# A two-block network on one core: loads of W and raw products spaced by task steps, 512-column pairs in the first expert matrix, a W build with two PSUM tiles per step, a later key transposition

## The chip, the cores and the metric

The kernel runs on one core of a Trainium2 chip. The metric is the device time of one execution in microseconds (us). Before the change three executions gave 3197.25, 3197.32 and 3201.41 us, a median of 3197.32 us. Engines are named as in the profile: PE (TensorE), PEld (its weight loads), DVE (VectorE), ACT (ScalarE), POOL (GpSimd), SP (SyncE, which here only issues DMAs).

## The reference, cut to what matters

256 tokens of width 2048 go through a block with stick-breaking attention and a squared-ReLU MLP, and then through a block with a pooled and a sparse attention, a product-key expert layer and a gate. All of it is float32. The change is in the second block, in its key projections and above all in the expert layer:

```
qkv, gates, u = split(rmsnorm(x) @ w_in)                   # keys are normed per head
q   = xn @ w_q                                             # 8 heads x 2 x 128
s   = einsum(q, sub_keys); top 16 x top 16 -> 16 experts per head and token: idx, g = softmax
h   = gelu(einsum('td,thkd->thk', xn, u_tab[idx]))         # u_tab: 16384 x 2048
out = einsum('thk,thkd->td', g * h, v_tab[idx])            # v_tab: 16384 x 2048
```

The kernel gathers nothing. It multiplies all 16384 experts with all tokens, and puts the routing weights g into a dense matrix W (16384 experts x 256 tokens, zero where an expert is not chosen): out = (W * gelu(xn u_tab^T)) v_tab.

## The kernel before

**Precision by splitting.** Every weight matrix comes in tiles of 128x2048 float32 (1 MB, tile name raw, three buffers). Each tile has two halves of 1024 columns. For each half ACT writes a rounded copy `hi` (L1431) and DVE, or in some stretches for every second half POOL, writes the rest `lo = raw - hi` (L1433); there are four buffers of hi and of lo. The left operand is split likewise (xh, xl, both in the tile xx). A product then is hi*xh + hi*xl + lo*xh, three passes over PE.

**Two shapes of product.** In `xs_half` (L240) the tokens are the stationary operand and 512 weight columns move; the accumulators are `acc`. In `ws_half` the weights are stationary, 128x128 at a time, and the tokens move; the accumulator is one PSUM bank named `ws`. `ws_half` has two forms. With `wide` unset, each of the 8 k-steps of a half issues three matmuls of 256 columns: hi on xh (L252), hi on xl (L253), lo on xh (L254). With `wide` set it issues one matmul of 512 columns (hi on xh and xl side by side, L250) and one of 256 (lo on xh, L254); the two halves of the bank are then added when it is emptied. The first MLP matrix (w1) uses the wide form already, the first expert matrix (peer_u, 128 items of one raw tile each) does not.

**What sets the order.** The order of the instructions of each engine is that in which the Python code issues them. The main loop walks over the halves. Before half n it issues hi and lo of half n+3 (`advance`); then the matmuls of half n. Twice in each half, in its middle and at its end, it calls `hook()`, in which each waiting task (a generator) goes on to its next `yield`. One such call is a **step** here, so a half has two. A half's load of a new raw tile is issued on SP as soon as the last lo of the tile in that buffer has been issued, so SP's queue holds it behind what was issued earlier.

**The expert layer's tasks**, all stepped that way:

- `u_item`: after the two halves of an item of peer_u, ACT copies its bank into a slot (L1264), 8 items to a slot; the slot is written to DRAM as raw product `gd` (L1270). Slots are ten buffers of 1 MB (names slot), handed out in the order in which they came free.
- `build`/`batch`: while peer_u runs, W is made from one-hot matrices, 8 tokens per batch, 32 batches, five steps apart. A batch is 16 matmuls of 128x128 in float16 into two `tp` banks (L1212), which ACT copies to a slot (L1216); two batches make a slot, which is written to DRAM as `wd` (L1221).
- `loader`: when W is complete, it reads for each of 16 groups of 1024 experts the piece of W and the raw products back into slots (L1232), both in one step, and marks the group as loaded 14 steps later. At most two groups are loaded and unused.
- `acts`: for a loaded group it multiplies by the norm factor (DVE L1281), applies gelu (ACT L1283), multiplies by W (DVE, two L1248), splits the result into ah (ACT L1291) and al (DVE L1293). These come one step after the other: DVE in one step, ACT in the next, DVE in the next.

The second expert matrix (peer_v) uses ah and al as stationary operand, in the form of L240, 16 groups after each other. `acts` of the first three groups run while peer_u is still being multiplied.

**The key transposition.** `kv_one` takes the accumulators of a key and value projection: DVE scales the keys into the tile xg (`spread`, L581), ACT copies the values (L615), and one step later PE transposes xg (L621).

**PSUM.** Eight banks are shared by kinds; `caps` says how many of each kind may be in use.

Of the kernel before, what the change touches and what calls it, by code (L numbers as in the profile page):

```python
# [19 lines left out]
P = 128  # L20
D = 2048
T = 256
# [4 lines left out]
def tile_two_blocks(ctx, tc, a, out):  # L27
    nc = tc.nc
    PE, ACT, DVE, POOL, SP = nc.tensor, nc.scalar, nc.vector, nc.gpsimd, nc.sync
# [10 lines left out]
    def f32(ap):  # L40
        return ap.bitcast(F32)

    live, caps = {}, {"acc": 4, "ws": 3, "tp": 3}
    idle, used = deque(range(8)), []

    def full(kind):
        return live.get(kind, 0) >= caps[kind] or kind in ("acc", "ws", "tp") and not idle

    def bank(kind):
        live[kind] = live.get(kind, 0) + 1  # L50
        i = idle.popleft()
        t = psp.tile([P, 512], F32, tag=f"bank{i}", name=kind)
        used.append((t, kind, i))
        return t

    def take(kind):
        while full(kind):
            hook()
        return bank(kind)

    def get(kind):
        while full(kind):
            yield
        return bank(kind)

    def tmp(pool, shape, dt, tag, cap):
        caps[tag] = cap
        while full(tag):
            yield
        live[tag] = live.get(tag, 0) + 1  # L70
        return pool.tile(shape, dt, tag=tag, name=tag, bufs=cap)

    def put(*kinds):
        for k in kinds:
            if not isinstance(k, str):
                u = next(u for u in used if u[0] is k)
                used.remove(u)
                idle.append(u[2])
                k = u[1]
            live[k] -= 1  # L80
# [18 lines left out]
    def S(ap, fn):  # L99
        seq.append(("s", ap, fn))  # L100
# [9 lines left out]
    st = {"rate": 2, "n": 0, "norm": 0, "rok": False, "pool_lo": False, "nb": 0, "nW": 0}  # L110
# [35 lines left out]
    def flush():  # L146
        until(lambda: st["norm"] == 0)
# [96 lines left out]
    def ws_half(hi, lo, k0, b, wide):  # L244
        xx, p = st["xx"], b[:, :T]
        for kk in range(8):
            k = k0 + kk
            c = slice(kk * P, (kk + 1) * P)
            if wide:
                PE.matmul(b, hi[:, c], xx[:, k].rearrange("p a t -> p (a t)"), start=k == 0, stop=False)  # L250
            else:
                PE.matmul(p, hi[:, c], xx[:, k, 0], start=k == 0, stop=False)  # L252
                PE.matmul(p, hi[:, c], xx[:, k, 1], start=False, stop=False)  # L253
            PE.matmul(p, lo[:, c], xx[:, k, 0], start=False, stop=k == 15)  # L254
            if kk == 3:
                hook()
# [18 lines left out]
    def ws_item(ap, evac, wide=False):  # L275
        box = {}

        def fn(j, hi, lo):
            if j == 0:
                box[0] = take("ws")  # L280
            else:
                flush()
            ws_half(hi, lo, 8 * j, box[0], wide)
            if j == 1:
                tasks.append(evac(box[0]))
        S(ap, fn)
# [276 lines left out]
    def rms64(tt, p, ng):  # L563
        sc = st["r"][:, tt:tt + 1]
        j0 = yield from tmp(ph["ew"], [P, 512], F32, "xn", 2)
        j = j0[:, :ng * 64]
        ACT.activation(j, p, AF.Square, scale=sc)
        yield
        r = smp.tile([P, 8], F32, tag="r64", name="r64", bufs=4)
        DVE.tensor_reduce(r[:, :ng], j.rearrange("p (g d) -> p g d", d=64), axis=AX.X, op=ALU.add)  # L570
        put("xn")
        DVE.tensor_scalar(r[:, :ng], r[:, :ng], 1.0 / 64, 1e-6, op0=ALU.mult, op1=ALU.add)
        yield
        POOL.tensor_tensor(r[:, :ng], r[:, :ng], mhalf[:, 0:1].to_broadcast([P, ng]), op=ALU.pow)
        yield
        DVE.tensor_scalar(r[:, :ng], r[:, :ng], sc, None, op0=ALU.mult)
        return r

    def spread(p, r):
        x = yield from tmp(smp, [P, 4, P], F32, "xg", 2)  # L580
        DVE.tensor_tensor(x.rearrange("p g (d e) -> p g d e", d=2),  # L581
                          p.rearrange("p (g e) -> p g e", g=4).unsqueeze(2).to_broadcast([P, 4, 2, 64]),
                          r.unsqueeze(2).unsqueeze(3).to_broadcast([P, 4, 2, 64]), op=ALU.mult)
        return x
# [25 lines left out]
    def kv_one(br, tt, p):  # L610
        while "E" not in done:
            yield
        r = yield from rms64(tt, p[:, :256], 4)
        x = yield from spread(p[:, :256], r[:, :4])
        ACT.activation(ph["VS"][:, tt, br], p[:, 256:], AF.Copy, scale=st["r"][:, tt:tt + 1])  # L615
        put(p)
        yield
        w = ph["qkw"][:, 1:2]
        b = yield from get("tp")
        for g in range(4):  # L620
            PE.transpose(b[:, g * P:(g + 1) * P], x[:, g], ident)  # L621
        put("xg")
        yield
        sl = (slice(None), br, slice(None), slice(tt * P, (tt + 1) * P))
        bv = b.rearrange("p (a b) -> p a b", a=4)
        ACT.activation(ph["kh"][sl], bv, AF.Copy, scale=w)
        yield
        DVE.scalar_tensor_tensor(ph["kl"][sl], bv, w, f32(ph["kh"][sl]), op0=ALU.mult, op1=ALU.subtract)
        put(b)
        done.add(("k", br, tt))  # L630
# [377 lines left out]
    def drop(nm):  # L1008
        del st[nm]
        w, i = held.pop(nm)  # L1010
        free[w].append(i)
# [181 lines left out]
    def batch(tb, h, S):  # L1193
        tm = ph["tm"]
        ts = slice(tb * 16 + h * 8, tb * 16 + h * 8 + 8)
        A = yield from tmp(tm, [P, 8, P], F16, "A", 2)
        DVE.tensor_tensor(A, ph["io16"].unsqueeze(1).to_broadcast([P, 8, P]),
                          ph["I2T"][:, ts].unsqueeze(2).to_broadcast([P, 8, P]), op=ALU.is_equal)
        yield
        eq = tm.tile([P, P, 8], F16, tag="eqb", name="eqb", bufs=1)  # L1200
        DVE.tensor_tensor(eq, ph["io8"], ph["I1T"][:, ts].unsqueeze(1).to_broadcast([P, P, 8]), op=ALU.is_equal)
        B = tm.tile([P, 2, P, 8], F16, tag="B", name="B", bufs=2)
        for m in range(2):
            DVE.tensor_tensor(B[:, m], eq, ph[f"G{m + 1}"][:, ts].unsqueeze(1).to_broadcast([P, P, 8]), op=ALU.mult)
            yield
        yield
        Sv = S.rearrange("p a t -> p (a t)").rearrange("p (i t) -> p t i", t=16)
        for k0 in (0, 4):
            bk = yield from get("tp")
            for k in range(4):  # L1210
                for m in range(2):
                    PE.matmul(bk[:, k * P:(k + 1) * P], B[:, m, :, k0 + k], A[:, k0 + k], start=m == 0, stop=m == 1)  # L1212
            if k0:
                put("A")
            yield
            ACT.copy(Sv[:, h * 8 + k0:h * 8 + k0 + 4], bk.rearrange("p (t i) -> p t i", t=4))  # L1216
            put(bk)
        st["nb"] = st.get("nb", 0) + 1
        st["nS", tb] = st.get(("nS", tb), 0) + 1
        if st["nS", tb] == 2:  # L1220
            SP.dma_start(st["wd"][:, :, tb].rearrange("g p c -> p g c"),  # L1221
                         S.rearrange("p a t -> p (a t)").rearrange("p (g c) -> p g c", g=16))
            drop(("S", tb))

    def loader():
        while "W" not in done:
            yield
        for g in range(16):
            while st["nW"] > 1 or nfree() < 2 + 2 * st["nW"] or ("u", g) not in done:
                yield  # L1230
            for nm, d in (("W", st["wd"][g].rearrange("p b c -> p (b c)")), ("ge", st["gd"][g])):
                SP.dma_start(grab((nm, g), keep=9).rearrange("p a t -> p (a t)"), d)  # L1232
            st["nW"] += 1
            for _ in range(14):
                yield
            done.add(("Wl", g))

    def wv(g, j0, n):
# [18 lines left out]
    def u_item(g, j):  # L1257
        def evac(b):
            if j == 0:
                while nfree() < 1:  # L1260
                    yield
                grab(("raw", g), keep=9)
            r = st["raw", g]
            ACT.copy(r[:, j], b[:, :T])  # L1264
            put(b)
            if j == 7:
                if g == 0:
                    st["gd"] = drp.tile([16, P, 8 * T], F32, name="gd")
                yield
                SP.dma_start(st["gd"][g], r.rearrange("p a t -> p (a t)"))  # L1270
                drop(("raw", g))
                done.add(("u", g))
        ws_item(a["peer_u"][8 * g + j], evac)

    def acts():
        for g in range(16):
# [281 lines left out]
```

## Time and profile before

| what | before |
|---|---|
| median of three executions | 3197.32 us |
| the profiled execution | 3201.31 us, span of the core 3199.6 us |
| PE busy | 3163.0 us, 99% of the span, 19145 matmuls |
| PEld busy | 2807.6 us (88%) |
| DVE, ACT, POOL busy | 1894.2, 1507.1, 409.2 us |
| mean granted clock of TensorE | 0.996 of full speed |
| peer_u, first to last matmul | 1592 to 2397 us |
| peer_v, first to last matmul | 2397 to 3096 us |
| DMA | 638.22 MB, 199 GB/s on average |

The profiled execution lies 4.0 us above the median. Its own time is 1.7 us longer than its span. Since matmuls are pipelined, a busy PE may still run below its pace: how fast it goes is read from the number of matmuls in a stretch.

### The profile page before, as it was taken

The page shows a single profiled execution, that of the slowest core. Times are in us where ns is not written, and L with a number is a line of the kernel's source. Part 1 is how long each engine was busy: PE and PEld are TensorE (multiplying, and loading weights), DVE is VectorE, ACT ScalarE, POOL GpSimd, SP SyncE. Part 2 cuts the span into 40 slices and gives each one's busy share as a digit, 9 for nine tenths or more (in the row PEclk, how much of TensorE's full clock was granted, in tenths as well). Part 3 has the DMA queues.
Part 4 walks back from the last instruction along what each step waited for, and adds up shares of the span by engine and source line. Part 5 has one row for each costly group of instructions (what it writes and reads, how often), then busy time and mean ns, then how long its engine had stood idle before and what let it go on. Part 6 is the DMA issues. An engine that isn't in the chain of part 4 may idle for free. (4 is left out here: it accounts for less than half of the span.)

```text
span 3199.6 us, 46639 instructions
## 1 busy us (share of the span) xinstructions
PE 3163.0 (99%) x19145; PEld 2807.6 (88%) x19145; DVE 1894.2 (59%) x2845; ACT 1507.1 (47%) x1984; POOL 409.2 (13%) x316
## 2 busy tenths in 40 slices
PE   9999999999999999999999999998999999999999
PEld 8999888888888878788999999988998888888887
DVE  6565565555656566466455655545446776777665
ACT  5444444444434544455444465644444444444443
POOL 0111000000001020000566533300000000000000
PEclk9999999999999999999999999999999999999999
DMA  6544555555555564235456677775656666666554
GB/s 214 179 162 169 196 184 188 194 185 194 187 191 189 186 201 150 106 132 184 171 190 209 208 238 234 239 258 206 209 198 233 240 249 237 248 227 248 200 180 163
DMA packets 121158, 638.22 MB, mean 199 GB/s; under 512 B 10263, under 2 KB 43047, under 8 KB 46832
## 3 DMA queue, kind: packets, MB, share of 16 engines
q1 hardware_dynamic: 119376, 629.58, 57.0%
q0 software_dynamic: 1424, 5.60, 0.8%
q8 instruction: 150, 2.46, 0.3%
q14 instruction: 64, 0.52, 0.1%
q10 hardware_dynamic: 144, 0.06, 0.0%
HBM read 598.76 MB, written 36.44 MB: 199 GB/s over the span
## 5 line engine op out<-in xcount | busy, mean ns | idle before, releaser
L1433 DVE TENSOR_TENSOR lo<-raw,hi 128x1024 fp32r<-128x1024 f32 x959 | 1188.8, 1245 | 1174.8 <-ACT hi L1431 1174.6
L1431 ACT ACTIVATE hi<-raw 128x1024 fp32r<-128x1024 f32 x1053 | 1106.7, 1056 | 779.5 <-PE acc L240 528.8
L254 PE MATMUL ws<-xx,lo 128*128 128x256 f32 x3840 | 1086.3, 283 | 10.3 <-DVE lo L1433 10.3
L252 PE MATMUL ws<-xx,hi 128*128 128x256 f32 x2816 | 807.6, 287 | 7.9 <-ACT hi L1431 7.8
L253 PE MATMUL ws<-xx,hi 128*128 128x256 f32 x2816 | 797.3, 283 | 0.1
L254 PEld LDWEIGHTS ws<-xx,lo 128*128 128x128 f32 x3840 | 733.6, 191 | 14.1 <-DVE lo L1433 13.9
L240 PE MATMUL acc<-hi,slot 128*128 128x512 f32 x2048 | 632.3, 389 | 0.0
L252 PEld LDWEIGHTS ws<-xx,hi 128*128 128x128 f32 x2816 | 540.7, 192 | 10.4 <-ACT hi L1431 10.1
L253 PEld LDWEIGHTS ws<-xx,hi 128*128 128x128 f32 x2816 | 540.8, 192 | 0.5 <-DVE xx L158 0.3
L240 PEld LDWEIGHTS acc<-hi,slot 128*128 128x128 f32 x2048 | 384.4, 188 | 79.7
L240 PE MATMUL acc<-lo,slot 128*128 128x512 f32 x1024 | 398.4, 389 | 0.0
L250 PE MATMUL ws<-xx,hi 128*128 128x512 f32 x1024 | 362.4, 399 | 0.3 <-DVE xx L158 0.3
L240 PE MATMUL acc<-hi,xx 128*128 128x512 f32 x960 | 315.9, 399 | 0.2 <-ACT hi L1431 0.2
L1433 POOL TENSOR_TENSOR lo<-raw,hi 128x1024 fp32r<-128x1024 f32 x94 | 234.4, 2495 | 285.0 <-ACT hi L1431 285.0
L250 PEld LDWEIGHTS ws<-xx,hi 128*128 128x128 f32 x1024 | 192.4, 188 | 48.3 <-DVE xx L158 0.6
L240 PEld LDWEIGHTS acc<-lo,slot 128*128 128x128 f32 x1024 | 192.2, 188 | 39.7
L240 PEld LDWEIGHTS acc<-hi,xx 128*128 128x128 f32 x960 | 183.0, 191 | 38.8 <-issue 1.0
L240 PE MATMUL acc<-hi,hh 128*128 128x512 f32 x512 | 199.8, 390 | 0.0
L240 PE MATMUL acc<-hi,hl 128*128 128x512 f32 x512 | 199.2, 389 | 0.0
L240 PE MATMUL acc<-lo,hh 128*128 128x512 f32 x512 | 199.2, 389 | 0.0
L240 PE MATMUL acc<-lo,xx 128*128 128x512 f32 x480 | 189.5, 395 | 1.3 <-DVE lo L1433 1.3
L1264 ACT COPY slot<-ws 128x256 f32<-128x256 f32 x128 | 47.6, 372 | 197.1 <-PE ws L254 191.5
(297 smaller groups left out, 2743.5 us busy)
## 6 DMA issues: line engine op xcount, KB each, us to landing
raw<-in_w_dram SPq DMA_DIRECT2D x128, 1024.0 KB, 4.8
raw<-in_peer_u_dram SPq DMA_DIRECT2D x128, 1024.0 KB, 5.0
raw<-in_peer_v_dram SPq DMA_DIRECT2D x128, 1024.0 KB, 4.8
raw<-in_wqk_dram SPq DMA_DIRECT2D x32, 1024.0 KB, 4.9
raw<-in_win_dram SPq DMA_DIRECT2D x28, 1024.0 KB, 4.8
raw<-in_wo_dram SPq DMA_DIRECT2D x16, 1024.0 KB, 4.8
raw<-in_wout_dram SPq DMA_DIRECT2D x16, 1024.0 KB, 4.8
raw<-in_peer_wq_dram SPq DMA_DIRECT2D x16, 1024.0 KB, 4.9
```

The lines of the kernel that those rows point to most:

```text
L240: PE.matmul(p, u, w, start=(k == first and i == 0), stop=(k == last and i == 2))
L250: PE.matmul(b, hi[:, c], xx[:, k].rearrange("p a t -> p (a t)"), start=k == 0, stop=False)
L252: PE.matmul(p, hi[:, c], xx[:, k, 0], start=k == 0, stop=False)
L253: PE.matmul(p, hi[:, c], xx[:, k, 1], start=False, stop=False)
L254: PE.matmul(p, lo[:, c], xx[:, k, 0], start=False, stop=k == 15)
L1264: ACT.copy(r[:, j], b[:, :T])
L1431: ACT.activation(hi[:, :nn], src, AF.Copy)
L1433: eng.tensor_sub(lo[:, :nn], src, f32(hi[:, :nn]))
```

## The change

The loader waits 14 steps after W is complete, and then issues the load of W and that of the raw products 12 steps apart, and marks the group as loaded 12 steps after the second. The items of peer_u use the wide form; their bank is emptied by an ACT copy of the right half and, one step later, a DVE addition of the left half. A batch of the W build takes its two banks at once and issues its 16 matmuls in one step; the two ACT copies follow in the next two steps, with a step after the second. `kv_one` waits three steps between scaling and transposing instead of one. Four instead of three banks may be of kind `ws`.

```
-    live, caps = {}, {"acc": 4, "ws": 3, "tp": 3}
+    live, caps = {}, {"acc": 4, "ws": 4, "tp": 3}
...
         put(p)
-        yield
+        for _ in range(3):
+            yield
         w = ph["qkw"][:, 1:2]
...
-        for k0 in (0, 4):
-            bk = yield from get("tp")
-            for k in range(4):
-                for m in range(2):
-                    PE.matmul(bk[:, k * P:(k + 1) * P], B[:, m, :, k0 + k], A[:, k0 + k], start=m == 0, stop=m == 1)
-            if k0:
-                put("A")
-            yield
+        bks = [(yield from get("tp")), (yield from get("tp"))]
+        for k in range(8):
+            for m in range(2):
+                PE.matmul(bks[k // 4][:, k % 4 * P:(k % 4 + 1) * P], B[:, m, :, k], A[:, k], start=m == 0, stop=m == 1)
+        put("A")
+        yield
+        for k0, bk in zip((0, 4), bks):
             ACT.copy(Sv[:, h * 8 + k0:h * 8 + k0 + 4], bk.rearrange("p (t i) -> p t i", t=4))
             put(bk)
+            yield
...
         while "W" not in done:
             yield
+        for _ in range(14):
+            yield
         for g in range(16):
...
                 SP.dma_start(grab((nm, g), keep=9).rearrange("p a t -> p (a t)"), d)
-            st["nW"] += 1
-            for _ in range(14):
-                yield
+                if nm == "W":
+                    st["nW"] += 1
+                for _ in range(12):
+                    yield
             done.add(("Wl", g))
...
             r = st["raw", g]
-            ACT.copy(r[:, j], b[:, :T])
+            ACT.copy(r[:, j], b[:, T:])
+            yield
+            DVE.tensor_add(r[:, j], r[:, j], b[:, :T])
             put(b)
...
-        ws_item(a["peer_u"][8 * g + j], evac)
+        ws_item(a["peer_u"][8 * g + j], evac, True)
```

SP's queue about the end of the W build, before: the last write of W is directly followed by the first two loads of the loader, and those by the raw tiles of peer_u.

```order
L1221 DMA wd<-slot_19582 128x16x128
L1405 DMA raw<-in_peer_u_dram 128x2048 x3
L1270 DMA gd<-slot_19424 128x2048
L1221 DMA wd<-slot_19790 128x16x128
L1232 DMA slot_20055<-wd 128x2048
L1232 DMA slot_20057<-gd 128x2048
L1405 DMA raw<-in_peer_u_dram 128x2048 x4
L1232 DMA slot_20272<-wd 128x2048
L1232 DMA slot_20274<-gd 128x2048
```

SP's queue at the same place with the change (L1222 is the write of W, L1235 the loader, L1276 the write of raw products, L1411 the raw tiles).

```order
L1222 DMA wd<-slot_18465 128x16x128
L1411 DMA raw<-in_peer_u_dram 128x2048 x2
L1276 DMA gd<-slot_18327 128x2048
L1222 DMA wd<-slot_18636 128x16x128
L1411 DMA raw<-in_peer_u_dram 128x2048 x4
L1235 DMA slot_19012<-wd 128x2048
L1411 DMA raw<-in_peer_u_dram 128x2048 x3
L1235 DMA slot_19149<-gd 128x2048
L1411 DMA raw<-in_peer_u_dram 128x2048
L1276 DMA gd<-slot_18851 128x2048
```

Four raw tiles now stand between the last write of W and its first load, and loads of a group are no longer next to each other.

ACT's queue and then DVE's queue in `acts` of the first group, before, with buffer numbers (a hi and the lo made from it can be matched by the number of hi). ACT:

```order
L1431 ACTIVATE hi_20321<-raw_20137 128x1024
L1291 ACTIVATE slot3_20340<-slot9_20057 128x512
L1431 ACTIVATE hi_20357<-raw_20197 128x1024
L1291 ACTIVATE slot3_20340<-slot9_20057 128x512
L1264 COPY slot6_20071<-ws_20327 128x256
L1431 ACTIVATE hi_20390<-raw_20197 128x1024
```

And DVE in the same piece, before:

```order
L1433 TENSOR_TENSOR lo_20322<-raw_20137,hi_20321 128x1024
L1248 SCALAR_TENSOR_TENSOR slot9_20057<-slot9_20057,slot8_20055 128x256 x2
L1433 TENSOR_TENSOR lo_20358<-raw_20197,hi_20357 128x1024
L1293 TENSOR_TENSOR slot5_20341<-slot9_20057,slot3_20340 128x512
L1248 SCALAR_TENSOR_TENSOR slot9_20057<-slot9_20057,slot8_20055 128x256 x2
L1433 TENSOR_TENSOR lo_20391<-raw_20197,hi_20390 128x1024
```

The two L1248 that feed the first L1291 stand after lo_20322; that L1291 stands before hi_20357. The same piece with the change (L1437 is hi, L1439 lo, L1297 the split of `acts` on ACT, L1299 that on DVE, L1252 the product with W, L1268 and L1270 the emptying of the bank), first ACT:

```order
L1437 ACTIVATE hi_19314<-raw_19176 128x1024
L1289 ACTIVATE slot6_19149<-slot6_19149 128x1024
L1437 ACTIVATE hi_19343<-raw_19223 128x1024
L1297 ACTIVATE slot2_19339<-slot6_19149 128x512
L1268 COPY slot7_19217<-ws_19320 128x256
L1437 ACTIVATE hi_19368<-raw_19223 128x1024
```

And DVE in the same piece, with the change:

```order
L1439 TENSOR_TENSOR lo_19315<-raw_19176,hi_19314 128x1024
L1270 TENSOR_TENSOR slot7_19217<-slot7_19217,ws_19270 128x256
L1252 SCALAR_TENSOR_TENSOR slot6_19149<-slot6_19149,slot9_19012 128x256 x2
L1439 TENSOR_TENSOR lo_19344<-raw_19223,hi_19343 128x1024
L1299 TENSOR_TENSOR slot3_19340<-slot6_19149,slot2_19339 128x512
L1252 SCALAR_TENSOR_TENSOR slot6_19149<-slot6_19149,slot9_19012 128x256 x2
L1439 TENSOR_TENSOR lo_19369<-raw_19223,hi_19368 128x1024
```

The two L1252 that feed the first L1297 now stand before lo_19344, while that L1297 stands after hi_19343: the product is issued one half earlier with respect to the split that reads it.

## Rows read from the trace of the kernel before

**Rows 1.** The page: the span, and PE's busy time, share and instructions.
```profile
span 3199.6 us, 46639 instructions
PE 3163.0 (99%) x19145; PEld 2807.6 (88%) x19145; DVE 1894.2 (59%) x2845; ACT 1507.1 (47%) x1984; POOL 409.2 (13%) x316
```

**Rows 2.** Windows by stage: length, busy of PE, PEld, DVE, ACT, POOL; clock; DMA.
```profile
1150.00:1160.00 10.00, 7.19 (x29) 5.62 (x29) 4.30 (x7) 4.11 (x6) 5.17 (x8) 0.83 0.76 268
1592.00:1822.00 230.00, 230.00 (x1920) 230.00 (x1919) 131.08 (x410) 97.81 (x131) 144.92 (x94) 1.00 0.59 202
1822.00:2095.00 273.00, 272.65 (x2468) 269.70 (x2467) 148.33 (x171) 161.81 (x187) 102.55 (x42) 1.00 0.74 236
2115.00:2215.00 100.00, 81.76 (x606) 75.84 (x606) 53.28 (x68) 43.70 (x58) 0.00 (x0) 0.97 0.61 225
2397.00:3199.60 802.60, 797.97 (x3536) 660.39 (x3534) 537.54 (x632) 367.05 (x400) 1.35 (x2) 1.00 0.62 222
```

**Rows 3.** Steady stretches of w1 (wide), peer_u (not wide) and peer_v.
```profile
950.00:1030.00 80.00, 80.00 (x455) 69.38 (x454) 50.37 (x71) 37.90 (x57) 8.59 (x14) 1.00 0.54 185
2250.00:2330.00 80.00, 80.00 (x669) 80.00 (x668) 33.89 (x28) 33.40 (x42) 0.00 (x0) 1.00 0.63 211
2500.00:2580.00 80.00, 80.00 (x355) 66.24 (x354) 57.04 (x69) 38.95 (x42) 0.00 (x0) 1.00 0.65 237
```

**Rows 4.** Timeline of PE about a W build group: start, length, line, tiles.
```profile
1848.34 0.71 PE L1212 MATMUL tp<-A,B 128*128 128x128 f16 x8
1848.86 0.36 PE L252 MATMUL ws<-xx,hi 128*128 128x256 f32 x1
1849.06 0.28 PE L253 MATMUL ws<-xx,hi 128*128 128x256 f32 x1
```

**Rows 5.** Waits of SP's queue, 2095 to 2215: total, times, longest.
```profile
SPq L1232 <- DMA wd<-slot: 11.7, 1, 11.7
```

**Rows 6.** Timeline of SP, two of its issues.
```profile
2096.48 0.38 SPq L1221 DMA_DIRECT2D wd<-slot  x1
2108.65 0.32 SPq L1232 DMA_DIRECT2D slot<-wd  x1
```

**Rows 7.** Waits on DMAs, 2080 to 2240: total, times, longest.
```profile
ACT hi L1431 <- DMA raw<-in_peer_u_dram: 8.0, 1, 8.0
ACT slot L1264 <- DMA gd<-slot: 5.6, 1, 5.6
```

**Rows 8.** Timeline of ACT in `acts` of the first group.
```profile
2141.63 0.63 ACT L1291 ACTIVATE slot<-slot 128x512 fp32r<-128x512 f32 x1 [2.63 <-DVE slot L1248]
2142.17 1.04 ACT L1431 ACTIVATE hi<-raw 128x1024 fp32r<-128x1024 f32 x1
```

**Rows 9.** Timeline of DVE in the same stretch.
```profile
2139.04 1.23 DVE L1433 TENSOR_TENSOR lo<-raw,hi 128x1024 fp32r<-128x1024 f32 x1 [1.92 <-ACT hi L1431]
2140.18 0.69 DVE L1293 TENSOR_TENSOR slot<-slot,slot 128x512 fp32r<-128x512 f32 x1
2140.78 0.76 DVE L1248 SCALAR_TENSOR_TENSOR slot<-slot,slot 128x256 f32<-128x256 f32 x2
2143.24 1.23 DVE L1433 TENSOR_TENSOR lo<-raw,hi 128x1024 fp32r<-128x1024 f32 x1 [1.71 <-ACT hi L1431]
```

**Rows 10.** Windows of 5 us: the lowest clock of the stretch.
```profile
2165.00:2170.00 5.00, 1.38 (x4) 1.09 (x5) 1.86 (x3) 1.33 (x2) 0.00 (x0) 0.64 0.02 7
```

**Rows 11.** Timelines of PE and DVE about the first key transposition.
```profile
1156.20 2.10 PE L621 MATMUL tp<-ident,xg 128*128 128x128 f32 x8 [2.81 <-DVE xg L581]
1156.43 0.69 DVE L581 TENSOR_TENSOR xg<-acc,r 128x512 f32<-128x512 f32 x1
```

**Rows 12.** Groups: the ACT copy of a bank half, the DVE addition in w1.
```profile
L1264 ACT COPY slot<-ws 128x256 f32<-128x256 f32 x128 | 47.6, 372 | 197.1 <-PE ws L254 191.5 <-DMA gd<-slot 5.6
L498 DVE TENSOR_TENSOR r<-r,ws 128x256 f32<-128x256 f32 x64 | 26.6, 415 | 0.0
```

## The prediction

> **What bounds the kernel now.** I read the page's busy shares first, then windows by stage, then the waits and timelines of the one stage that falls behind. PE is busy for 3163.0 of 3199.6 us [rows 1], so only two things can move the time: how long PE needs for its matmuls, and the few stretches in which it falls behind its pace. Pace is read from counts. In a steady stretch of the first expert matrix PE starts 669 matmuls in 80 us, which is one per 0.120 us or 0.359 us for a k-step of three; in w1, which has the wide form already, it starts 455 in 80 us, which is 227.5 pairs of 0.352 us; in peer_v 355 of 512 columns, 0.225 us each [rows 3]. Against that pace the stages show two holes [rows 2]. From 2115 to 2215 PE starts 606 matmuls where 836 (669 x 100/80) fit: 230 are missing, worth 230 x 0.120 = 27.5 us, though only 18.2 us show as idle. From 1150 to 1160 it starts 29, and the clock there is 0.83. In peer_v and behind it (2397 to the end) PE is busy for 798.0 of 802.6 us: what the loader does there stays hidden.
>
> **The first hole and its causes.** Three things meet in it. First, SP is a queue: the load of the first group's W had to wait 11.7 us for the last write of W [rows 5], from its write at 2096.48 to 2108.65 [rows 6], and four raw tiles stood behind it. ACT then waited 8.0 us for a raw tile [rows 7]. Second, a raw-product slot was filled again at once, so ACT waited 5.6 us for its write to DRAM [rows 7]; in between the granted clock was 0.64 over 5 us, part of them at 1.2 instead of 2.4 GHz, with PE idle for most of that window [rows 10]. Third, and dearest, the tasks of `acts` form a ring with hi and lo. In ACT's queue L1291 stands before the next hi, and it needs L1248, which in DVE's queue stands behind the lo of the hi before. So within one half run, one after the other: hi 1.04, lo 1.23, L1293 0.69, two L1248 0.76, L1291 0.63 us [rows 8, 9], and one turn takes 2143.24 - 2139.04 = 4.20 us [rows 9], while PE needs 24 x 0.120 = 2.88 us for a half. Each turn loses 1.3 us; a group has about six turns, and three groups follow each other with only two halves between them. The lead is three halves, less the 2.3 us that hi and lo take themselves: 3 x 2.88 - 2.3 = 6.3 us, and it was gone after the raw tile's delay.
>
> **The change part by part.**
>
> The wide form: 128 items x 16 k-steps = 2048 k-steps, each now 0.352 instead of 0.359 us. By the counts that is 2048 x 0.0071 = 14.5 us; I take 14. Bounds: nothing, if the pair does no better here than three passes; at the other end 0.120 us plus 0.225 us (the matmul of peer_v) = 0.345 us a pair, 28 us. The row nearest is w1, which is the same code on the same shapes.
>
> On this one place the Trainium skill speaks with another size: "TensorE: Matmul & The Clock Gate", section Back-to-back issue gap, gives N/2.4 + 2.5 ns at full clock for the isolated gap. An estimate by that page is 3 x 109 = 327 ns against 216 + 109 = 325 ns, 2.5 ns a k-step and 5 us in all; the trace shows 359 and 352 ns, so it does not agree with that formula for three weight loads in a row, and I stay with the counts.
>
> Emptying the bank: the ACT copy is as long as before, 372 ns; new are 128 DVE additions of 415 ns [rows 12], 53 us of DVE. DVE is busy for 131 of 230 and 148 of 273 us in the two stretches of peer_u before the hole [rows 2]; one addition in two halves (5.64 us) adds 7%, so 54% becomes 62%. PE covers it: I take nothing. Without that cover it costs 53 us (rivals). The bank is free about a microsecond later; the fourth `ws` bank covers that.
>
> The W build: the same 512 matmuls and 64 copies. A group of eight holds PE for 1848.86 - 1848.34 = 0.52 us, and the matmul behind it starts 0.20 instead of 0.12 us before the next, so 0.60 us [rows 4]. With sixteen in one place one of two such borders goes, some 0.05 us, 32 times: 1 us gained, with 0 and 3 us (32 x 0.08) as bounds. The queue of ACT keeps its order. A batch now needs two banks at once, and a step without them moves only the batch.
>
> The key transposition: PE reached L621 at 1156.20 - 2.81 = 1153.39 and waited 2.81 us; the second xg was written at 1156.43 + 0.69 = 1157.12 [rows 11]. Of the 29 starts in the window [rows 2] 21 are matmuls of 0.225 us, 4.7 us, and 8 are transposes, some 1 us (between the 0.52 us of eight L1212 [rows 4] and the 2.10 us here): 5.7 us of work in 10 us, 4.3 us lost. Two steps are one half of 12 matmuls, 2.7 us. PE then arrives at 1156.1, about when the first xg is there, and still waits some 0.6 us for the second. I take 3 us gained; bounds 0 (what it waits for comes later too) and 4.3 us. The hi and lo of the halves after it are not fed by L621; next late is DVE's xg itself.
>
> The loader: three effects. Four raw tiles, some 23 us, now stand between the last write of W and its load, twice the 12.2 us that the load waited for that write, so SP is not held there, and the raw tiles are not. W and raw products of a group arrive 12 steps or 17 us apart, and the groups of `acts` have five to seven halves between them instead of two, in which the lead comes back (2.82 us a half against 1.2 us for the longer of hi and lo). And the ring opens: the tasks of `acts` start 14 + 24 - 14 steps later for the loader, and one for the batch's added step, 25 in all. That is odd, so what stood at a half's end now stands in its middle. The queues with the change show it: the products L1252 that feed the first split on ACT stand one lo earlier than before. A turn then holds DVE for lo, L1293, two L1252 and half an addition, by the starts 1.14 + 0.60 + 0.76 + 0.21 = 2.7 us [rows 9, 12], below the 2.82 us of a half; ACT's 1.04 + 0.63 + 0.19 us run beside it. What is late next is the refill of a raw slot, once, as before: it can hold ACT for some 2 to 6 us, within the lead of 6 us. Of 27.5 us I leave 4 us: gained 23.5. Bounds: 0 (all three come back) and 27.5 us. In peer_v a half is 24 x 0.225 = 5.4 us against a turn of 4.2 us: hidden before and after.
>
> The sum against the profiled execution: 3201.3 - 14 - 1 - 3 - 23.5 = 3159.8 us. That execution stands 4.0 us above the median; if these 4 us lie in the first hole, the median comes to 3160 too, else to 3156. I take 3158 us.
>
> **The rivals.**
>
> The hole only moves (14%). The refilled slot or a load behind a write on SP delays hi in the midst of `acts`, and half of the 27.5 us stays. For it: ACT's 5.6 us; the third group's loads again stand beside the write of raw products. Against it: the lead is whole when they come. Time: 3158 + 13 = 3171 us.
>
> The wide pair gains a third of what it does in w1, because beside `acts` or the W build the weight load of the 256-column pass shows more than in w1 (6%): 14 x 2/3 = 9 us stay, 3158 + 9 = 3167 us. The formula cited above would come out there.
>
> The spacing does nothing (5%): `acts` keeps the ring, because the parity of the steps is made even by a step in which the loader waits for a slot. Then only 14 + 1 + 3 us go: 3197.3 - 18 = 3179 us.
>
> Slower than before (4%): the DVE addition. It stands in DVE's queue between the lo of the halves and waits for an ACT copy that waits for PE. If by it DVE's work between two additions exceeds the 5.64 us of an item, every item is late by 0.42 us, 53 us in all: 3158 + 53 = 3211 us. It decides from a DVE share of 100% in peer_u; with 62% it is far from it.
>
> **How the numbers follow.** The forecast has 71%, with 3150 to 3167 us as its own range (all of the hole and 4 us of the keys gone; or 9 us more left). The range that holds 8 in 10 reaches into the moved hole: 3148 to 3173 us. About 0.2% (6.4 us) is what a measurement of this kernel can tell from no change; only the last rival and a part of unforeseen waits lie above 3191 us. Faster 0.92, within 0.04, slower 0.04.
>
> **What would show it.** In the profile after: some 455 matmuls in 80 us in peer_u; peer_u about 765 us long instead of 805; no 11.7 us wait of SP for the write of W; in `acts` of the first groups hi every 2.8 us instead of 4.2; no window with a clock of 0.64 there; PE's wait before the first L621 below 1.5 us. Wrong would be a PE that misses over 100 matmuls in any 100 us of peer_u, or DVE's addition as the releaser of PE.

## The result and the profile after

The changed kernel took 3157.85 us (median of four runs, 3156.42 to 3160.24) against 3198.00 us before: ratio 0.9873, 95% interval 0.9856 to 0.989. The time is the predicted one; the parts of the sum are not, and errors of opposite sign hide each other. The profiled execution took 3158.02 us, 43.3 us less than that of before. Its lines are numbered as in the queues with the change; L1289 is the gelu and L1287 the norm factor ahead of it.

The page of the kernel after, its line of engines, answers to [rows 1]: PE is as full as before, with 2048 matmuls fewer.

```profile
PE 3129.0 (99%) x17097; PEld 2684.7 (85%) x17097; DVE 1971.4 (62%) x2973; ACT 1505.3 (48%) x1984; POOL 415.1 (13%) x316
```

Windows of the kernel after, for [rows 2] and [rows 3]: busy us and starts of PE, PEld, DVE, ACT and POOL, then the granted clock and the DMAs. In order: w1, the first hole, late peer_u, and all from peer_v on. A window's count takes in the two or three matmuls that reach over its edges, so counts of windows of one length are compared.

```profile
950.00:1030.00 80.00, 80.00 (x455) 69.31 (x454) 49.94 (x71) 38.33 (x58) 8.96 (x15) 1.00 0.52 185
2115.00:2215.00 100.00, 96.29 (x541) 83.51 (x540) 67.21 (x92) 53.37 (x69) 0.00 (x0) 0.97 0.69 246
2250.00:2330.00 80.00, 80.00 (x464) 69.93 (x463) 42.57 (x47) 36.17 (x45) 0.00 (x0) 1.00 0.61 214
2341.50:3156.30 814.80, 802.12 (x3538) 659.78 (x3536) 537.89 (x633) 367.14 (x400) 1.35 (x2) 1.00 0.59 219
```

Three readings. An undisturbed 100 us at the hole holds 579 starts (later loads, below), so the hole still misses 38, which are 38 x 100/579 = 6.6 us instead of 27.5. Late peer_u starts 464 matmuls in 80 us where w1, in the same form, starts 455. And from peer_v to the end the kernel needs 814.8 us, where it needed 802.6 before [rows 2]: 12 us lost in a part that the prediction called hidden.

The bank copies of peer_u (ACT) give its length: count, ns min/median/max, first and last start, in the kernel after.

```profile
L1268 ACT COPY slot<-ws x128: 350/372/375, 1592.7 to 2341.7; 128x256 f32<-128x256 f32 x128
```

Before they ran from 1598.7 to 2397.0 us. So the 43.3 us are 6.0 gained ahead of peer_u, 49.3 in it (749.0 against 798.3 us), and 12 lost behind it.

The ring is open in the first groups, as forecast. ACT of the kernel after, within the first group: start, length, line, form, and idle time ahead with its releaser.

```profile
2130.58 1.06 ACT L1437 ACTIVATE hi<-raw 128x1024 fp32r<-128x1024 f32 x1
...
2132.58 1.06 ACT L1437 ACTIVATE hi<-raw 128x1024 fp32r<-128x1024 f32 x1
2134.00 0.64 ACT L1297 ACTIVATE slot<-slot 128x512 fp32r<-128x512 f32 x1 [0.35 <-DVE slot L1252]
...
2135.69 1.06 ACT L1437 ACTIVATE hi<-raw 128x1024 fp32r<-128x1024 f32 x1
```

The hi copies stand 2.0 and 3.1 us apart (2130.58, 2132.58, 2135.69), not 4.2 us [rows 9], and the split on ACT waits 0.35 us for the products instead of 2.63 [rows 8].

What is left of the hole is one refill: ACT waits for a slot whose raw products are still on their way to DRAM. SP and ACT of the kernel after, then three windows of 5 us there (columns as above).

```profile
2160.61 0.42 SPq L1235 DMA_DIRECT2D slot<-wd  x1
2161.08 0.42 SPq L1276 DMA_DIRECT2D gd<-slot  x1
```
```profile
2173.30 0.37 ACT L1268 COPY slot<-ws 128x256 f32<-128x256 f32 x1 [10.54 <-DMA gd<-slot]
```
```profile
2165.00:2170.00 5.00, 5.00 (x31) 4.39 (x30) 0.00 (x0) 0.00 (x0) 0.00 (x0) 1.00 0.96 310
2170.00:2175.00 5.00, 1.75 (x10) 1.27 (x8) 0.33 (x1) 1.70 (x3) 0.00 (x0) 0.87 0.15 61
2175.00:2180.00 5.00, 4.53 (x14) 3.48 (x14) 5.00 (x9) 4.04 (x7) 0.00 (x0) 0.50 0.56 206
```

The write was issued right behind a load of W, and the two moved together: the DMA engines were busy for 0.96 of the window from 2165. ACT stood still for 10.5 us, more than the lead of 6 us. PE ran dry, and in the 5 us after that the granted clock was 0.50, the lower of its two levels (1.2 GHz), so that 14 matmuls started in a window nearly full.

In peer_v, PE waits once in each of twelve groups. The waits view of PE from 2341 to 3100 us: total, times, longest; then ACT ahead of one of these places.

```profile
PE acc L240 <- DVE lo L1439: 7.8, 12, 0.7
```
```profile
2425.82 1.06 ACT L1289 ACTIVATE slot<-slot 128x1024 f32<-128x1024 f32 x1 [2.43 <-DVE slot L1287]
2426.78 3.11 ACT L1437 ACTIVATE hi<-raw 128x1024 fp32r<-128x1024 f32 x3
...
2438.01 1.04 ACT L1437 ACTIVATE hi<-raw 128x1024 fp32r<-128x1024 f32 x1
2441.62 0.63 ACT L1297 ACTIVATE slot<-slot 128x512 fp32r<-128x512 f32 x1 [2.57 <-DVE slot L1252]
2442.16 1.05 ACT L1437 ACTIVATE hi<-raw 128x1024 fp32r<-128x1024 f32 x1
```

The ring is closed here: a turn takes 2442.16 - 2438.01 = 4.15 us, while PE needs 12 x 0.225 = 2.7 us for a half. Four turns cost 4 x 1.45 = 5.8 us of lead. Ahead of them stand three hi copies in one row (2426.78): ACT is still catching up after the gelu when the split begins.

### The profile page after: what moved, and what is told of

It reads as the page before. It is cut to its first block, busy times and chain, and to the rows that moved or that the text cites. A ratio compares the mean times of both kernels' runs of the same rounds, so it can differ in the third digit from the quotient of the medians.

```text
span 3156.3 us, 42670 instructions
## 1 busy us (share of the span) xinstructions
PE 3129.0 (99%) x17097; PEld 2684.7 (85%) x17097; DVE 1971.4 (62%) x2973; ACT 1505.3 (48%) x1984; POOL 415.1 (13%) x316
## 4 chain that ended last, share of the span: by engine, by line
PE 96%; DVE 2%; DMA 1%; ACT 1%; issue 0%; POOL 0%; SPq 0%; DVEq 0%; ACTq 0%; POOLq 0%
PE acc L240 48%; PE ws L250 22%; PE ws L254 14%; PE ws L253 3%; PE ws L252 3%; DVE lo L1439 1%; PE tp L1212 1%; PE tp L866 1%; PE tp L173 0%; PE acc L712 0%; ACT hi L1437 0%; DMA gd<-slot 0%; PE ws L834 0%; PE ws L784 0%; PE tp L854 0%
## 5 line engine op out<-in xcount | busy, mean ns | idle before, releaser
L1439 DVE TENSOR_TENSOR lo<-raw,hi 128x1024 fp32r<-128x1024 f32 x959 | 1197.9, 1254 | 1042.3 <-ACT hi L1437 1042.0
L1437 ACT ACTIVATE hi<-raw 128x1024 fp32r<-128x1024 f32 x1053 | 1107.3, 1057 | 772.2 <-PE acc L240 531.0
L250 PE MATMUL ws<-xx,hi 128*128 128x512 f32 x3072 | 1079.9, 397 | 3.5 <-ACT hi L1437 3.2
L254 PE MATMUL ws<-xx,lo 128*128 128x256 f32 x3840 | 1075.0, 280 | 0.7 <-DVE lo L1439 0.5
L250 PEld LDWEIGHTS ws<-xx,hi 128*128 128x128 f32 x3072 | 577.6, 188 | 138.6 <-ACT hi L1437 3.6
L1439 POOL TENSOR_TENSOR lo<-raw,hi 128x1024 fp32r<-128x1024 f32 x94 | 239.0, 2544 | 261.5 <-ACT hi L1437 261.3
L252 PE MATMUL ws<-xx,hi 128*128 128x256 f32 x768 | 220.6, 287 | 0.0
L253 PE MATMUL ws<-xx,hi 128*128 128x256 f32 x768 | 217.3, 283 | 0.1
L253 PEld LDWEIGHTS ws<-xx,hi 128*128 128x128 f32 x768 | 147.1, 192 | 0.5 <-DVE xx L158 0.3
L252 PEld LDWEIGHTS ws<-xx,hi 128*128 128x128 f32 x768 | 147.1, 192 | 0.2
L1268 ACT COPY slot<-ws 128x256 f32<-128x256 f32 x128 | 47.6, 371 | 199.7 <-PE ws L254 189.2
```

Of the source, the lines that this page charges most:

```text
L1268: ACT.copy(r[:, j], b[:, T:])
L1437: ACT.activation(hi[:, :nn], src, AF.Copy)
L1439: eng.tensor_sub(lo[:, :nn], src, f32(hi[:, :nn]))
```

## The experiments

Each is the changed kernel with one edit (both repairs together have two), executed four or five times. Beside its time, a median, stands its own ratio to before with the interval; the changed kernel has 0.9873 (0.9856 to 0.989). The kernel before had medians of 3198.0, 3199.9 and 3200.6 us in the three series (the changed kernel, the first four experiments, the last four), so a difference of medians between series is uncertain by 2 to 3 us. The intervals of the old loader, of the key step, of the build and of the later loads alone touch or overlap that of the changed kernel; there the stretch decides and not the time. Up to peer_u single executions differ by up to 4 us, so stretches are compared by their own lengths.

**The narrow form back.**

```
-            ACT.copy(r[:, j], b[:, T:])
-            yield
-            DVE.tensor_add(r[:, j], r[:, j], b[:, :T])
+            ACT.copy(r[:, j], b[:, :T])
             put(b)
+            yield
...
-        ws_item(a["peer_u"][8 * g + j], evac, True)
+        ws_item(a["peer_u"][8 * g + j], evac)
```

> The changed kernel with the first expert matrix put back to the narrow form (three matmuls of 256 columns per k-step, no DVE addition when its bank is emptied); everything else as changed. Theory A (the wide form brought about twice what the prediction gave it): a step of peer_u goes back from 0.346 us to 0.360 us, that is 0.014 us on 2048 steps, +28 us, so about 3186 us, and windows of 5 us in peer_u hold fewer matmul pairs of work. Rival B (the prediction's 14 us was right and the rest of the shortening of peer_u has another cause, such as fewer stalls): about 3172 us.

3181.24 us, 0.9944 (0.993 to 0.9957): 23.4 us above the changed kernel, nearer to theory A. Windows of this kernel, the hole and late peer_u:

```profile
2115.00:2215.00 100.00, 97.77 (x800) 97.36 (x800) 54.88 (x62) 48.97 (x64) 0.00 (x0) 0.98 0.72 254
2250.00:2330.00 80.00, 80.00 (x669) 80.00 (x669) 36.50 (x30) 34.58 (x44) 0.00 (x0) 1.00 0.63 217
```
The pace is that of [rows 3] again, 669 in 80 us, and from first to last bank copy peer_u is 771.9 us long (1592.5 to 2364.4), 22.9 more than with the wide form. The hole misses 36 matmuls of 0.120 us, 4.3 us, so with narrow matmuls too all but this is gone: the wide form did not mend the hole. The fourth `ws` bank is kept here; what it brings by itself was not tried.

**The old loader.**

```
-        for _ in range(14):
-            yield
         for g in range(16):
...
-                if nm == "W":
-                    st["nW"] += 1
-                for _ in range(12):
-                    yield
+            st["nW"] += 1
+            for _ in range(14):
+                yield
```

> The changed kernel with the loader as it was before: no 14 steps ahead of it, the load of W and the load of the raw products in one step, 14 steps after both. Theory A (what matters for peer_u is the step in which the activation's instructions stand, mid-half or end of half, and in this kernel they stand mid-half as in the changed one; and the slow second expert matrix comes from the spacing): hi copies beside the activations of the first groups follow each other at 2.7 to 3 us and not at 4.2 us, peer_u loses at most 8 us more than in the changed kernel, mostly because SP waits again for the write of W, and peer_v takes 699 us instead of 710.6; about 3147 to 3155 us. Rival B (the spacing itself is what removed the stall): PE's stall of some 27 us about the first groups is back, peer_u about 19 us longer, peer_v 11.7 us shorter: about 3165 us.

3147.81 us, 0.9842 (0.9829 to 0.9856): theory A, 10 us faster than with the new loader. The waits of SP's queue in this kernel, 2060 to 2130 us, and then its windows there and about the hole:

```profile
SPq L1233 <- DMA wd<-slot: 10.9, 1, 10.9
```
```profile
2070.00:2120.00 50.00, 50.00 (x294) 43.80 (x293) 32.05 (x42) 29.42 (x37) 2.40 (x1) 1.00 0.89 331
2115.00:2215.00 100.00, 95.43 (x542) 82.95 (x541) 63.87 (x82) 50.04 (x65) 0.00 (x0) 0.98 0.68 243
```

SP's wait for the write of W is back, 10.9 us, and PE loses nothing by it: 50.00 of 50 us busy around it, with 294 starts. The hole is as small as with the new loader (542 against 541 starts); it again is one refill, for which ACT waited 10.6 us. So the spacing is not what removed the hole. Of what could move the activations into the middle of a half, only the added step of a batch is left in this kernel; one without that step was not run. From the last bank copy of peer_u to the end it takes 802.9 us, as before the change.

**13 steps instead of 14.**

```
-        for _ in range(14):
+        for _ in range(13):
```

> The changed kernel with 13 instead of 14 steps of waiting before the loader's first load, and nothing else. Theory A (the odd or even step decides: with an odd shift the instructions of the activation stand at the end of a half and not in its middle, right between the hi of one half and the hi of the next, so that ACT and DVE wait for each other in turn): beside the activations of the first three groups hi copies follow each other at 4.2 us, the lead is lost in each of them, peer_u is 8 to 20 us longer, the whole 3166 to 3178 us. Rival B (only the distance from the write of W and from each other matters, one step more or less does not): the same time, 3156 to 3160 us, hi copies at 2.7 us.

3172.63 us, 0.9916 (0.9902 to 0.9929): 14.8 us lost by one step, theory A. ACT of this kernel in the first group:

```profile
2138.53 1.06 ACT L1437 ACTIVATE hi<-raw 128x1024 fp32r<-128x1024 f32 x1
2142.22 0.63 ACT L1297 ACTIVATE slot<-slot 128x512 fp32r<-128x512 f32 x1 [2.62 <-DVE slot L1252]
2142.75 1.04 ACT L1437 ACTIVATE hi<-raw 128x1024 fp32r<-128x1024 f32 x1
```

With all the spacing in place the ring is closed: 4.22 us from hi to hi, and 2.6 us of waiting for the products, as before the change. Here 76 starts are missing from 2115 to 2215 (503 of 579, 13 us) against 38. The next 100 us, in this kernel and then in the changed one, hold the larger part of the loss:

```profile
2215.00:2315.00 100.00, 94.90 (x525) 81.24 (x524) 54.60 (x64) 44.06 (x57) 0.00 (x0) 0.98 0.62 220
```
```profile
2215.00:2315.00 100.00, 100.00 (x579) 87.45 (x578) 52.99 (x58) 45.35 (x58) 0.00 (x0) 1.00 0.68 245
```

Another 54 starts, 9.3 us, go here. In the third group the ring is closed too, and ACT waits a second time for a slot that is still being written to DRAM, so PE runs dry again:

```profile
2229.71 0.37 ACT L1268 COPY slot<-ws 128x256 f32<-128x256 f32 x1 [2.84 <-DMA gd<-slot]
```

With the lead whole, 2.84 us would be within it; about 1 us of the 9.3 is the slower pace of pairs told at the end. Peer_u is 16.7 us longer (765.7 against 749.0), of which this execution made up 3 us ahead of it. This and the old loader, taken together, show the cause of the hole: the place in the half.

**Loads of a group in one step, from the fifth group on.**

```
-                for _ in range(12):
+                if g < 4:
+                    for _ in range(12):
+                        yield
+            if g > 3:
+                for _ in range(14):
                     yield
```

> The changed kernel, but from the fifth group on the loader issues the load of W and that of the raw products in one step and waits 14 steps after them, as before the change; the first four groups keep the new spacing. Theory A (the spacing of 12 and 12 steps puts the two gelu instructions of a group so close ahead of its four split turns that the lead of hi and lo is used up once in each group of the second expert matrix): the waits of PE for lo of about 1 us, once in each group, go, peer_v takes about 699 us instead of 710.6, the whole about 3146 us. Rival B (the longer peer_v has another cause, for instance the position of the chain in the half): peer_v stays at 710 us, the whole at 3158 us.

3149.97 us, 0.984 (0.9827 to 0.9854): theory A. A window of peer_v in the changed kernel, then in this one, and ACT in this one (L1441 is hi here, L1301 the split):

```profile
2400.00:2700.00 300.00, 296.10 (x1299) 243.15 (x1298) 211.52 (x257) 139.00 (x148) 0.00 (x0) 1.00 0.62 235
```
```profile
2400.00:2700.00 300.00, 300.00 (x1326) 248.48 (x1325) 215.52 (x262) 142.00 (x152) 0.00 (x0) 1.00 0.65 239
```
```profile
2433.13 1.06 ACT L1441 ACTIVATE hi<-raw 128x1024 fp32r<-128x1024 f32 x1 [1.66 <-PE acc L240]
...
2436.70 1.04 ACT L1441 ACTIVATE hi<-raw 128x1024 fp32r<-128x1024 f32 x1
2440.30 0.63 ACT L1301 ACTIVATE slot<-slot 128x512 fp32r<-128x512 f32 x1 [2.56 <-DVE slot L1256]
2440.84 1.04 ACT L1441 ACTIVATE hi<-raw 128x1024 fp32r<-128x1024 f32 x1
```

The ring is as closed as before (4.14 us a turn, the split at the same steps), but the hi ahead of the first turn waits for PE (2433.13): the lead is whole when the split begins, and four turns don't use it up. From the last bank copy of peer_u to the end it is 802.9 us again. So the distance between gelu and split costs the 12 us, not the ring alone. The whole is only 7.9 us shorter by the medians, because this execution's peer_u is 4 us longer than that of the changed kernel (753.1 us), for the most part by a longer wait ahead of the build and by the slower pace of pairs behind the hole.

**One step before the key transposition.**

```
-        for _ in range(3):
-            yield
+        yield
```

> The changed kernel with one step, as before, instead of three between scaling and transposing the keys. Theory A (the prediction's): PE waits again some 2.8 us before the first key transposition, the window from 1150 to 1160 us holds about 29 instead of 48 matmuls, and the time is 3 to 4 us longer, about 3161.5 us. Rival B (the wait only comes back at another place, or the 4 us before the first expert matrix are from something else): 3158 us, within 1 us of the changed kernel.

3163.06 us, 0.9883 (0.9868 to 0.9898): 3 us longer by the ratios, 5 us by the medians; what the time can't settle the window does. 1120 to 1180 us after, then in this kernel, and its PE there:

```profile
1120.00:1180.00 60.00, 59.40 (x273) 48.76 (x272) 41.74 (x61) 30.14 (x43) 16.09 (x19) 1.00 0.62 205
```
```profile
1120.00:1180.00 60.00, 57.31 (x256) 46.62 (x255) 39.62 (x59) 27.74 (x40) 15.56 (x19) 0.97 0.56 190
```
```profile
1154.70 2.09 PE L621 MATMUL tp<-ident,xg 128*128 128x128 f32 x8 [2.29 <-DVE xg L581]
```

17 starts of 0.225 us are gone, 3.8 us, and a wait of 2.29 us is back. Theory A.

**Eight matmuls per step in the W build** (with the step at the end of a batch kept).

```
-        bks = [(yield from get("tp")), (yield from get("tp"))]
-        for k in range(8):
-            ...
-        for k0, bk in zip((0, 4), bks):
+        for k0 in (0, 4):
+            bk = yield from get("tp")
+            ...
+            yield
             ACT.copy(Sv[:, h * 8 + k0:h * 8 + k0 + 4], bk.rearrange("p (t i) -> p t i", t=4))
             put(bk)
-            yield
+        yield
```

> The changed kernel with the W build as before, eight matmuls and one bank per step, but with the added step at the end of a batch kept, so that all later steps stand as in the changed kernel. Theory A (the prediction's: one border of a group of float16 matmuls costs 0.05 us, 32 of them go): 1 us longer, within 0 and 3 us, about 3159 us. Rival B (the fewer groups matter more, since the longer pair hides less of a border): over 5 us longer, above 3163 us.

3163.63 us, 0.9888 (0.9872 to 0.9903): 5.8 us longer by the medians, where theory B begins, and 4.8 us by the ratios; either is above what A allows. The build's own share has to be read from its stretch. PE of the changed kernel about a batch, then of this one:

```profile
1906.76 1.21 PE L1212 MATMUL tp<-A,B 128*128 128x128 f16 x16
1907.78 0.47 PE L250 MATMUL ws<-xx,hi 128*128 128x512 f32 x1
...
1908.21 0.40 PE L250 MATMUL ws<-xx,hi 128*128 128x512 f32 x1
```
```profile
1901.11 0.71 PE L1213 MATMUL tp<-A,B 128*128 128x128 f16 x8
1901.64 0.47 PE L250 MATMUL ws<-xx,hi 128*128 128x512 f32 x1
...
1902.07 0.40 PE L250 MATMUL ws<-xx,hi 128*128 128x512 f32 x1
```

Eight hold PE for 0.53 us and sixteen for 1.02 us, and the pair behind either takes 0.43 instead of 0.35 us. Two groups of eight cost 2 x (0.53 + 0.08) = 1.22, one of sixteen 1.10 us: 0.12 us, 32 times, 3.8 us. From the 40th to the 90th bank copy, which holds the build, this kernel needs 316.6 and the changed one 312.9 us: 3.7 us. That lies between the two theories. The rest belongs to no part of the edit that is seen here: peer_u as a whole is 9.6 us longer (758.6 us), the 5.9 us outside the build going with the slower pace of pairs told at the end, and this execution reached peer_u 3.4 us earlier.

**Later loads for the third and fourth group**, alone, and then with the loads in one step from the fifth group on.

```
                 yield
+            for _ in range({2: 8, 3: 2}.get(g, 0)):
+                yield
             for nm, d in (("W", st["wd"][g].rearrange("p b c -> p (b c)")), ("ge", st["gd"][g])):
```

> The changed kernel with the loads of the third group 8 steps later and those of the fourth 2 steps later, so that the slot whose raw products are just being written to DRAM is not the next one that ACT fills; the steps of all activations keep their place in the half. Theory A (the rest of the hole is that one refill, for which ACT waited 10.5 us): no wait of ACT for the write of gd above 1 us, no window of 5 us in peer_u before 2330 with fewer than 28 matmuls, 8.6 us gone: about 3149.5 us. Rival B (the wait moves: the load of W now takes that slot, so SP's queue waits for the write, and the raw tiles behind it come late, or the next slot is refilled at once): 3156 to 3160 us.

> The changed kernel with both repairs: the loads of a group in one step from the fifth group on, and the later loads of the third and the fourth group. If the two losses, 8.6 us in the first hole and 8 to 11.7 us in the second expert matrix, lie in different stretches, they add up: 3138 to 3142 us. If they share a cause or if one comes back as the other goes: 3147 to 3150 us.

Alone 3153.49 us, 0.9853 (0.9838 to 0.9868), 4.4 us faster than the changed kernel; both together 3141.25 us, 0.9815 (0.9802 to 0.9828), the fastest kernel here, 16.6 us below the changed one and 59.4 us below before. The window of the hole in the first, then one of peer_v in both together:

```profile
2115.00:2215.00 100.00, 100.00 (x579) 87.49 (x578) 67.34 (x88) 55.44 (x70) 0.00 (x0) 1.00 0.76 271
```
```profile
2400.00:2700.00 300.00, 300.00 (x1325) 248.51 (x1324) 214.32 (x262) 139.62 (x150) 0.00 (x0) 1.00 0.66 245
```

The hole is gone in either (578 starts in the second) and no wait of ACT for gd is left. Theory A of the first holds for the mechanism; its 8.6 us were too many: the full pace here is 579, so the stall was 6.6 us, and peer_u is only 4.0 us shorter (745.0 us), because this execution had lost 2.6 us in it before by the pace of pairs. The two losses lie in different stretches and add up: with both edits peer_u takes 744.9 us, and the part behind it 802.8 us.

## Why the prediction came out, point by point

The time was within 0.2 us of the median. That is luck: the errors of the parts cancel. In us gained:

| term | predicted | measured |
|---|---|---|
| wide form | 14 | 25.2 (22.9 in peer_u, though its hole is 2.3 larger) |
| W build | 1 | 3.8 (border) |
| key transposition | 3 | 3.8 (window) |
| first hole | 23.5 | 20.9 (27.5 less 6.6 left) |
| peer_v | 0 | -12 |
| sum | 41.5 | 41.7 |

The profiled executions differ by 43.3 us; the 1.6 us beyond the sum lie ahead of the keys, and are of the size by which single executions differ there.

**The wide form** was mis-sized. I took w1's pair as the nearest row, since it is the same code on the same shapes. In peer_u a pair takes 0.347 us (923 starts in 160 us, last section), near the other bound of 0.345 us, the sum of two rows. At w1's pace the term would have come out; why the same pair goes faster in peer_u stays open (last section). The formula of the Trainium skill that was weighed there ("TensorE: Matmul & The Clock Gate", section Back-to-back issue gap), which the page gives for the isolated gap, does not fit these runs either: an estimate by it makes the form worth 5 us and a pair 325 ns, where 347 and 353 ns are measured.

**The first hole** had three named causes, and the runs weigh them anew. The ring is the dear one, as said, and the parity of the step opens it, as said (13 against 14 steps). SP's wait for the write of W cost nothing by itself in an open ring (old loader), and the wider gaps between the groups brought nothing that can be seen in the hole (542 starts without them, 541 with). I had expected the refilled slot to hold ACT for 2 to 6 us, within the lead; it held it for 10.5 us, and 6.6 us are left instead of 4. With that the sign named for the clock failed as well: a window of 5 us with 0.50 is there. The rival in which half of the hole stays for that reason had the mechanism right and the size too large.

**The step that failed** is the last sentence on the loader: "In peer_v a half is 24 x 0.225 = 5.4 us against a turn of 4.2 us: hidden before and after." A half of peer_v is 12 matmuls, 2.7 us; 24 is the count of a narrow half of peer_u. I used the right figure, 2.7 us for a half of 12 matmuls, at the keys. With it the ring in peer_v loses 1.45 us a turn, and before the change it was hidden only because the first half of the split stood eight halves behind the gelu, in which the lead came back. With the new spacing it stands three behind it (2426.78 above). ACT of the kernel before, from the second gelu of a group to the first split:

```profile
2468.43 1.06 ACT L1283 ACTIVATE slot<-slot 128x1024 f32<-128x1024 f32 x1 [2.43 <-DVE slot L1281]
2469.39 2.94 ACT L1431 ACTIVATE hi<-raw 128x1024 fp32r<-128x1024 f32 x3
...
2484.02 1.07 ACT L1431 ACTIVATE hi<-raw 128x1024 fp32r<-128x1024 f32 x1 [1.66 <-PE acc L240]
2487.05 0.63 ACT L1291 ACTIVATE slot<-slot 128x512 fp32r<-128x512 f32 x1 [1.96 <-DVE slot L1248]
```

Eight hi copies lie between the two, and the last of them waits for PE.

**The keys and the DVE addition** went as forecast: PE's wait is 0.3 us instead of 2.81 [rows 11], and DVE's addition is no releaser of PE in peer_u; what PE waits there for DVE's lo is at most 0.5 us.

## What to carry to other kernels

Where two in-order queues feed each other, look at which instruction stands ahead of which before looking at how long anything takes: one step of a half decided 15 us here, and a spacing of loads that looked like the remedy cost 12. Count the matmuls of a half in the very stage that the sentence is about. And a buffer handed out in the order of release is refilled at once when the pool is nearly empty: ask which write is still reading it.

## What the runs showed that I had not expected

The same pair of matmuls runs at two steady paces. In the changed kernel itself w1 has 455 starts in 80 us and late peer_u 464, both with PE busy without a gap. From 1630 to 1790 us, in peer_u, three kernels that are identical up to there in their program differ in the same way: the changed one, then that with later loads alone, then that with the loads of a group in one step.

```profile
1630.00:1790.00 160.00, 160.00 (x923) 140.54 (x922) 120.61 (x337) 69.00 (x92) 106.85 (x72) 1.00 0.63 217
```
```profile
1630.00:1790.00 160.00, 159.80 (x907) 138.34 (x906) 105.87 (x336) 67.84 (x89) 104.44 (x71) 1.00 0.61 212
```
```profile
1630.00:1790.00 160.00, 159.81 (x922) 140.47 (x921) 113.91 (x337) 68.95 (x92) 106.53 (x73) 1.00 0.62 217
```

923 starts in 160 us are 0.347 us a pair, 907 are 0.353 us. The changed kernel has no gap here; the second has one of 0.2 us, and the slower pace behind it; the third has a gap of 0.2 us at the same place and goes on at the faster pace. So a short idle moment alone does not decide it. 16 starts are 2.8 us. The clock is 1.00 in all three. What switches the pace was not tried and stays open; it moves single executions by about 2 to 6 us in peer_u.
